# Scores over 192 keys in two query halves, tiles at multiples of 64 bytes, and a new order in the opening of a one-core transformer layer

## The chip, the cores and the metric

The kernel runs on one core of one Trainium2 chip. The metric is the device time of one execution in microseconds (us), as the median of several executions. The kernel before takes 1698.69 us (median of 3, 1698.04 to 1703.2).

## The reference, cut to what matters

One layer over 2048 tokens of width 1024. `c` sets a shift, a scale and a gate per channel; the input is modulated, multiplied by one wide matrix, cut into eight pieces, and two token mixers (windowed attention with sinks, and a causal pool) are gated, added, projected and normalised.

```python
mod = jax.nn.silu(c) @ w_ada[l] + b_ada[l]               # 1024 -> 3 * 1024
shift, scale, gate = jnp.split(mod, 3, axis=-1)
u = x * (1.0 + scale[:, None, :]) + shift[:, None, :]
q, k, v, a_gate, p_in, p_gate, m_a, m_p = jnp.split(u @ w_in[l], offsets, axis=-1)
# attention: 16 query heads, 2 key heads, head width 64; query i sees keys i-127 .. i
logits = q k^T / 8 + bias[bucket(i - j)];  masked outside the window
probs = softmax(concat(logits, sink_of_head))[..., :-1]   # the sink takes weight, has no value
a = (probs @ v) * silu(a_gate) @ w_attn_proj
p = (group_linear(pool(p_in)) * pool_scale) * silu(p_gate) @ w_pool_proj
y = (sigmoid(m_a) * a + sigmoid(m_p) * p) @ w_out * (1 + gate)
x = LayerNorm(alpha * x + y)
```

The kernel is given float32 and keeps about that precision: each operand of a product is split into a rounded part and the rest ("hi" and "lo", type fp32r), and three matmuls (hi*hi, hi*lo, lo*hi) stand for one.

## The kernel before, in words

**Products.** Every large product of the layer is a 2x2 block product done with seven block products instead of eight (Strassen's way, in Winograd's form). The seven names of the moving operand are B11, T1, T2, B21, T3, B22 and T4; each is a set `set_<name>` in SBUF of 4 pieces of 128 rows by 512 columns, hi and lo. A `Quad` is one 2x2 block product: two weight matrices of 128 columns each over 1024 rows against 1024 tokens. Its weights go through four stages, F (B11, T1), S (T2, B21), Th (T3, B22) and L (T4). Each of the seven products is `product()`: 4 pieces times 3 matmuls, 12 matmuls of 128x512 on TensorE, which accumulate in a PSUM bank (`mm`, or `lg` and `c` for pairs of quads). A weight is split by a cast on ScalarE (`w_set<-W`, CAST) and a subtraction on VectorE (`w_set<-W,w_set`); GpSimd forms the sums of weights (`W<-W`).

**Phases.** The tokens are done in two halves, s = 0 and 1. For each half: a start phase (`g0`, `g1`) with the quads for keys/values, the first queries and two gates; the phase "alone" (`o0`, `o1`), in which 13 quads run one after another and the attention is laid over them; and an end phase (`e0`, `e1`), in which pool jobs are laid over four pairs of quads. Then come the projections, `w_out` and the LayerNorms.

**What sets the order.** `plan()` writes all products down in one list and places the loads and the splits of weights some products ahead; `run()` walks it, and `at`, `defer` and `steps` hang other work at a position in it. All engines run in that program order; the tile framework adds the waits. Each engine has one queue, SyncE (SP) issues nearly all DMAs.

**Attention in "alone".** `overlay()` cuts it into 128 steps a layer (64 for each half of the tokens: 8 pairs of heads times 8 blocks of 128 queries). `step(n)` is called after every 4.7 groups of three matmuls or so and does parts of four steps at once: the score matmuls of step n (`scores`: for each of two heads, hi and lo, 128 queries against 256 keys, into the only `lg` bank), the four transposes of step n-2 into the only `pt` bank, and the four matmuls with the values of step n-3 (`pv`). Behind them ScalarE divides the weights of step n-1 by their sum, casts `pt` to `pth`, copies half of `pv` to `o`, and takes two exponentials; VectorE takes a reciprocal, adds bias and takes the minimum with the sink (`CUSTOM_DVE_ANT_0 L<-lg,bt,nsink`), then forms `ptl<-pt,pth`, then adds the two halves of `pv`. The transposes of a step must wait until the `ptl` of the step before has read the one `pt` bank. `load_q` fetches the queries of two steps, two steps ahead, from `q_d`; `q_quad.consume` writes `q_d` from a ring of 5 (4 in the second half) tiles of the tag `c`.

**The opening.** `head()` writes the order of the first two quads (keys/values and queries, F and S) out by hand. A row of `mod` for 128 channels comes in two ways: shifts on TensorE (`pe_modulation`: eight matmuls with one moving column, "a list" below), scales on VectorE (`modulation`: `head_T<-head_T,cb,mod` over 1024 elements), which needs `cb`, silu(c) on every partition. `cb` is c read by a broadcasting DMA, put through tanh on ScalarE and two operations of VectorE. For channel tiles 0 to 3 that gives B11 and T1, for 4 to 7 B21 and T2; from them come T3, B22 and T4. `idle_products` are matmuls on constants that keep TensorE's clock up. Then `first_start` lays 16 "folds" over the rest of the phase (`fold_parts`: the pool's mix matrix times the pool's columns of `w_in`, 12 matmuls of 128x256 each), and the gates' rows of `mod` (`gate_modulation`).

The lines of most instructions in the profile are one helper's (L56), so groups are told apart by their tiles' names.

## Time and profile before

| what | us |
| --- | --- |
| median of three executions | 1698.69 |
| the profiled execution, device time | 1703.35 |
| its span in the trace | 1701.2 |
| TensorE busy | 1665.3 |
| VectorE, ScalarE, GpSimd busy | 1185.1, 988.4, 589.4 |

Up to about 161 us the start phase of the first half runs, from 161 to 480 us the first "alone" phase, from 740 to 1060 us the second; the rest are phases without attention. The PE rows count a matmul from its start until its result is out, so the times of matmuls that follow each other overlap: the group row's busy time divided by its count is what one of them costs in a row of its kind.

### The profile page before, as it was taken

Reading aid. Unit: us, or ns where it says so; the run is one execution under the profiler, and the core shown is the slowest. Engines: PE = TensorE matmul, PEld = TensorE weight load, DVE = VectorE, ACT = ScalarE, POOL = GpSimd, SP = SyncE. Lnnn points to the kernel's source line nnn. Section 1 sums busy time; section 2 is a strip of 40 time slices with the busy share of each in tenths; the row PEclk is TensorE's granted clock in tenths of the full one; section 3 lists DMA queues with packets and bytes.
Section 4 is the critical chain, followed back from the end, with each engine's and each line's share of the span. In section 5 each row is a group of like instructions: output and inputs, shape, how many; then the busy total and the mean of one; then the engine's idle time right before and its main releaser. Section 6 shows DMA issues by size and latency. Waiting matters only on the chain.

```text
span 1701.2 us, 24948 instructions
## 1 busy us (share of the span) xinstructions
PE 1665.3 (98%) x8112; PEld 1397.0 (82%) x8112; DVE 1185.1 (70%) x2167; ACT 988.4 (58%) x1943; POOL 589.4 (35%) x563
## 2 busy tenths in 40 slices
PE   9899999999999999999999999999999999999997
PEld 7788888888788888888888888888888888888886
DVE  6855666666647778656666666487876785778878
ACT  4645888787853336358877787333544453434553
POOL 3013454545462223323424333322242211113544
PEclk9899999999999999999999999999999999999999
DMA  9489676776557889865456454589968685777343
GB/s 358 151 294 311 202 225 217 242 239 208 170 178 223 264 288 326 289 206 157 150 171 215 156 175 135 190 280 326 329 238 309 197 312 201 261 264 281 149 149 124
DMA packets 236833, 389.50 MB, mean 229 GB/s; under 512 B 20872, under 2 KB 90528, under 8 KB 236576
## 3 DMA queue, kind: packets, MB, share of 16 engines
q1 hardware_dynamic: 231280, 382.36, 66.8%
q10 hardware_dynamic: 5392, 5.53, 1.0%
q8 instruction: 64, 1.05, 0.3%
q14 instruction: 65, 0.53, 0.1%
q0 software_dynamic: 32, 0.02, 0.0%
HBM read 243.63 MB, written 147.35 MB: 230 GB/s over the span
## 4 chain that ended last, share of the span: by engine, by line
PE 68%; ACT 11%; DVE 6%; issue 5%; DMA 3%; POOL 1%; SPq 1%; DVEq 0%; ACTq 0%; POOLq 0%
PE mm L56 43%; PE lg L56 11%; PE c L56 9%; ACT L L56 5%; PE pv L56 3%; PE pt L56 3%; DVE w_set L56 2%; ACT pth L56 2%; ACT w_set L56 1%; DVE wide L56 1%; ACT sig L56 1%; DVE p L56 1%; DVE ptl L56 1%; SPq L56 1%; ACT q_hi L56 0%
## 5 line engine op out<-in xcount | busy, mean ns | idle before, releaser
L56 PE MATMUL mm<-set_B,w_set 128*128 128x512 f32 x2664 | 652.7, 391 | 0.6 <-DVE w_set L56 0.6
L56 PEld LDWEIGHTS mm<-set_B,w_set 128*128 128x128 f32 x2664 | 496.6, 188 | 103.7 <-DVE w_set L56 1.5
L56 PE MATMUL mm<-set_T,w_set 128*128 128x512 f32 x1896 | 466.1, 392 | 1.5 <-POOL w_set L56 1.2
L56 POOL TENSOR_TENSOR W<-W 128x512 f32<-128x512 f32 x185 | 266.9, 1453 | 573.1 <-DVE w_set L56 394.0
L56 PEld LDWEIGHTS mm<-set_T,w_set 128*128 128x128 f32 x1896 | 351.5, 189 | 74.4 <-POOL w_set L56 2.5
L56 DVE TENSOR_TENSOR w_set<-W,w_set 128x1024 fp32r<-128x1024 f32 x197 | 254.5, 1292 | 110.5 <-ACT w_set L56 109.2
L56 ACT ACTIVATE L<-L 128x257 f32<-128x257 f32 (+3 forms) x512 | 241.4, 498 | 96.8 <-DVE L L56 96.3
L56 ACT CAST w_set<-W 128x1024 fp32r<-128x1024 f32 x222 | 232.2, 1047 | 97.2 <-PE mm L56 54.2
L56 PE MATMUL lg<-set_T,w_set 128*128 128x512 f32 x828 | 201.0, 391 | 2.7 <-ACT lg L56 1.7
L56 PE MATMUL c<-set_T,w_set 128*128 128x512 f32 x828 | 200.8, 391 | 0.0
L56 PEld LDWEIGHTS lg<-set_T,w_set 128*128 128x128 f32 x828 | 155.4, 188 | 36.2 <-ACT lg L56 2.1
L56 PEld LDWEIGHTS c<-set_T,w_set 128*128 128x128 f32 x828 | 155.8, 189 | 32.2
L56 DVE TENSOR_TENSOR ptl<-pt,pth 128x512 fp32r<-128x512 f32 (+1 forms) x128 | 86.4, 675 | 112.6 <-ACT pth L56 112.6
L56 POOL TENSOR_TENSOR W<-W,A 128x512 f32<-128x512 f32 x41 | 57.9, 1412 | 275.1 <-DMA A<-in_win_dram 102.7
L56 DVE CUSTOM_DVE_ANT_0 L<-lg,bt,nsink 128x256 f32<-128x256 f32 (+1 forms) x256 | 110.1, 467 | 25.1 <-PE lg L56 20.9
L56 ACT ACTIVATE sig<-mm 128x512 f32<-128x512 f32 x76 | 45.5, 599 | 94.6 <-PE mm L56 92.5
L56 PEld LDWEIGHTS lg<-kk,qs 128*128 128x128 f32 x512 | 77.4, 189 | 15.4 <-DVE L L56 4.6
L56 PE MATMUL pt<-ident,L 128*128 128x128 f32 x496 | 76.7, 276 | 9.3 <-DVE ptl L56 8.8
L56 PE MATMUL lg<-kk,qs 128*128 128x256 f32 (+1 forms) x512 | 81.5, 281 | 2.2 <-DVE L L56 1.9
L56 POOL TENSOR_TENSOR w_set<-W,w_set 128x1024 fp32r<-128x1024 f32 x25 | 61.0, 2441 | 63.7 <-ACT w_set L56 37.5
L56 PE MATMUL pv<-pth,vv 128*128 128x256 f32 x248 | 74.8, 323 | 1.1 <-DMA vv<-v_d 1.1
L56 DVE TENSOR_TENSOR st<-pv,o 64x128 f32<-64x128 f32 x256 | 71.3, 279 | 5.5 <-ACT o L56 3.8
(207 smaller groups left out, 1884.2 us busy)
## 6 DMA issues: line engine op xcount, KB each, us to landing
W<-in_win_dram SPq DMA_DIRECT2D x40, 512.0 KB, 5.8
qs<-q_d SPq DMA_DIRECT2D x128, 128.0 KB, 4.3
sums_d<-W SPq DMA_DIRECT2D x62, 256.0 KB, 4.1
W<-sums_d SPq DMA_DIRECT2D x31, 512.0 KB, 4.2
ain_d<-st SPq DMA_DIRECT2D x56, 256.0 KB, 3.5
A<-in_win_dram SPq DMA_DIRECT2D x42, 256.0 KB, 5.6
q_d<-q_hi SPq DMA_DIRECT2D x32, 256.0 KB, 4.4
q_d<-q_lo SPq DMA_DIRECT2D x32, 256.0 KB, 4.2
```

The lines of the kernel that those rows point to most:

```text
L56: return lambda *args, **kw: self.tc.keep_in_program_order(op(*args, **kw))
```

## The change

**Scores.** A block of 128 queries of two heads is no longer taken as two heads of 128 queries, but as two halves of 64 queries, each with both heads stacked on the 128 partitions. A half needs only 192 keys (`BAND`): keys 0 to 191 of the window's 256 for the first half, 64 to 255 for the second. So the four score matmuls of a step have 192 columns in place of 256 (in the first block of the sequence 64 and 128 in place of 128), and bias-and-minimum, exponential and division work on 192 or 193 columns in place of 256 or 257. The bias tile is 192 wide and loaded by two DMAs, the sink is one value per partition. The transposes and the matmuls with the values keep their size: the 64 columns that a half doesn't use are zeroed once for each of three fixed rooms for `L`. `q_d` is laid out in blocks of 64 queries, so that its DMAs move pieces of 64 floats.

**Tiles.** A room for `L` is 528 floats in place of 518, so the tiles allocated behind it start at multiples of 64 bytes.

**Seeds.** In the end phases both accumulators of the first pair get a matmul that opens the bank (one more for each of two phases).

**Opening.** `cb` is made on TensorE (silu(c)'s columns, broadcast as weights, against the identity) and copied by ScalarE; the DMA, the tanh and two VectorE operations for it go. The scales of channel tiles 5 and 6 are done on TensorE as well. The hand-written order of F and S is another, the Th products of the first two quads are woven (T3, T3, B22, B22 in place of T3, B22, T3, B22), some consumers of these quads come up to five products later (`LATER`), and the 16 folds start four products later; the last eight come two to a product.

```diff
-    nsink = cp.tile([P, HEADS], F32, name="nsink")
+    nsink = cp.tile([P, 2 * KT], F32, name="nsink")[:, :KT]
...
-    q_d = dp.tile([2, KT, 2, 2, P, CH], F32, name="q_d")
+    q_d = dp.tile([2, KT, 2, 2, CH // HD, P, HD], F32, name="q_d")
...
-            self.fresh = True
+            self.fresh = {0, 1} if "pg" in bufs else {1}
...
+                    if kind == "Th" and gi == 0 and phase.get("woven"):
...
+                        products += [(q, kind, h, name) for h, name in enumerate(names) for q in grp]
+                        continue
...
+    LATER = {(0, "S"): 5, (1, "S"): 4, (1, "Th"): 5, (1, "L"): 2}
...
+    def keep_q(dst, x):
+        sp.dma_start(dst.rearrange("b p c -> p b c"), x.rearrange("p (b c) -> p b c", c=HD))
...
+        rooms = [tp.tile([P, 2 * 257 + 14], F32, tag=f"L{i}", bufs=1, name="L") for i in range(3)]
+        for room in rooms:
+            pool.memset(room[:, 1 + BAND : 1 + BAND + P], 0.0)
...
-            q = qts[h] = tp.tile([P, 2, 2 * P], F32R, tag="qs", bufs=2, name="qs")
+            q = qts[h] = tp.tile([P, 4, 2, HD], F32R, tag="qs", bufs=2, name="qs")
             for n in range(2):
-                src = q_d[s, j, t, n][:, c * 2 * P : (c + 1) * 2 * P].rearrange("(h d) c -> d h c", h=2)
-                sp.dma_start(as32(q[n * HD : (n + 1) * HD]), src)
+                src = q_d[s, j, t, n, 4 * c : 4 * c + 4].rearrange("b (h d) c -> d (b h) c", h=2)
+                sp.dma_start(as32(q[n * HD : (n + 1) * HD]).rearrange("p b h c -> p (b h) c"), src)
...
+        def span_of(n, eo):
+            k0 = k0_of(n)
+            return (max(k0, HD), 2 * P) if eo else (k0, BAND)
...
         def scores(n):
...
-            for h in range(2):
+            for eo in range(2):
+                whi = q[:, n % 2 * 2 + eo].rearrange("p h c -> p (h c)")
+                k0, k1 = span_of(n, eo)
                 for hl in range(2):
                     mm(
-                        lg[:, h, k0:],
-                        q[:, h, at : at + P],
-                        kvt["k"][:, hl, (b - 1 + s) * P + k0 : (b + 1 + s) * P],
+                        lg[:, eo, k0:k1],
+                        whi,
+                        kvt["k"][:, hl, (b - 1 + s) * P + k0 : (b - 1 + s) * P + k1],
...
-                        L[:, h, e0:256],
-                        lg[:, h, e0:],
-                        bts[j][:, h, e0:],
+                        L[:, a:c],
+                        lg[:, eo, k0:k1],
+                        bts[j][:, k0 - HD * eo : k1 - HD * eo],
...
+                    with_sink = L[:, a : c + 1] if eo else L[:, a - 1 : c]
...
-        sp.dma_start(cb, c.partition_broadcast(P))
...
-        act.activation(late[0], cb, AF.Tanh, scale=0.5)
-        dve.tensor_scalar(late[0], late[0], 0.5, 0.5, ALU.mult, ALU.add)
-        dve.tensor_tensor(cb, cb, late[0], ALU.mult)
+        for h in range(2):
+            row = bank(("pv", "pt")[h])
+            for i in range(KT // 2):
+                k = h * (KT // 2) + i
+                mm(row[:, i * P : (i + 1) * P], ct[:, k : k + 1].to_broadcast([P, P]), ident, start=i == 0, stop=True, skip_group_check=True)
+            act.copy(cols(cb, h), row)
...
+    PE_SCALE = (5, 6)
...
+            for n in range(2 if k in PE_SCALE else 1):
+                for i in range(KT):
+                    at_i = slice(i * P, (i + 1) * P)
+                    mm(sums[k][:, n : n + 1], ws[k][n][:, at_i], ct[:, i : i + 1], start=i == 0, stop=i == KT - 1)
```

The first place is TensorE in `head()`, where the S products of the first pair begin (`lg` and `c` with T2, `mm` with B21; the rows `ct,head_...` are the lists, eight matmuls with one moving column each; the two single rows with 128x512 open the banks). Before:

```order
L56 MATMUL mm<-set_B_66,w_set 128x512 x3
L56 MATMUL mm<-set_T_67,w_set 128x512 x3
L56 MATMUL pv<-ct,head_big 128x1 x8
L56 MATMUL lg<-set_B_66 128x512
L56 MATMUL c_463<-set_B_66 128x512
L56 MATMUL lg<-set_T_159,w_set 128x512 x3
L56 MATMUL mm<-set_B_68,w_set 128x512 x3
L56 MATMUL pt<-ct,head_big_112 128x1 x8
L56 MATMUL c_463<-set_T_159,w_set 128x512 x3
```

And after the change:

```order
L56 MATMUL mm<-set_B_66,w_set 128x512 x3
L56 MATMUL mm<-set_T_67,w_set 128x512 x3
L56 MATMUL lg<-set_B_66 128x512
L56 MATMUL c_435<-set_B_66 128x512
L56 MATMUL pt<-ct,head_B_116 128x1 x16
L56 MATMUL pv<-ct,head_big 128x1 x16
L56 MATMUL lg<-set_T_159,w_set 128x512 x3
L56 MATMUL mm<-set_B_68,w_set 128x512 x3
L56 MATMUL c_435<-set_T_159,w_set 128x512 x3
L56 MATMUL mm<-set_B_68,w_set 128x512 x3
L56 MATMUL pt<-ct,head_big_112 128x1 x8
```

Four lists (two tiles, shift and scale) now stand in one block between the last F product and the first S product, where one list of tile 6 stood; the list of tile 5 stood between F products.

The second place is TensorE behind it, the Th and L products of the first pair (T3 is `set_T_406` before and `set_T_411` after, B22 `set_B_565` and `set_B_459`, T4 `set_T_621` and `set_T_613`; `vt` rows transpose the values, `spare,room_w` rows are folds). Before:

```order
L56 MATMUL lg<-set_T_406,w_set 128x512 x12
L56 MATMUL mm<-set_B_565,w_set 128x512 x12
L56 MATMUL pt<-ident,vt 128x128 x4
L56 MATMUL c_463<-set_T_406,w_set 128x512 x12
L56 MATMUL pv<-spare,room_w 128x256 x12
L56 MATMUL mm<-set_B_565,w_set 128x512 x12
L56 MATMUL pt<-spare,room_w 128x256 x12
L56 MATMUL lg<-set_T_621,w_set 128x512 x12
L56 MATMUL pv<-spare,room_w 128x256 x12
L56 MATMUL c_463<-set_T_621,w_set 128x512 x12
L56 MATMUL pt<-spare,room_w 128x256 x12
L56 MATMUL pv<-ident,vt 128x128 x4
```

And after:

```order
L56 MATMUL lg<-set_T_411,w_set 128x512 x12
L56 MATMUL c_435<-set_T_411,w_set 128x512 x12
L56 MATMUL mm<-set_B_459,w_set 128x512 x12
L56 MATMUL pt<-ident,vt 128x128 x4
L56 MATMUL mm<-set_B_459,w_set 128x512 x12
L56 MATMUL lg<-set_T_613,w_set 128x512 x12
L56 MATMUL c_435<-set_T_613,w_set 128x512 x12
L56 MATMUL pv<-ident,vt 128x128 x4
```

No fold stands here any more, and one more product stands between the first T3 product and the first transposes of `vt`.

The third place is TensorE at the start of the first "alone" phase. Before:

```order
L56 MATMUL lg<-kk,qs 128x128 x4
L56 MATMUL mm<-set_T_406,w_set 128x512 x9
L56 MATMUL mm<-set_B_565,w_set 128x512 x6
L56 MATMUL lg<-kk,qs 128x256 x4
L56 MATMUL mm<-set_B_565,w_set 128x512 x6
```

And after:

```order
L56 MATMUL lg<-kk,qs 128x64 x2
L56 MATMUL lg<-kk,qs 128x128 x2
L56 MATMUL mm<-set_T_411,w_set 128x512 x9
L56 MATMUL mm<-set_B_459,w_set 128x512 x6
L56 MATMUL lg<-kk,qs 128x192 x4
L56 MATMUL mm<-set_B_459,w_set 128x512 x6
```

The products and the places of the steps among them are the same; only the width of the score matmuls differs.

## The prediction

> **What bounds the kernel now.** I read the page's totals first, then the busy times by stage, then what TensorE waited for, then the rows of the opening in order of time.

> ```profile
> PE 1665.3 (98%) x8112; PEld 1397.0 (82%) x8112; DVE 1185.1 (70%) x2167; ACT 988.4 (58%) x1943; POOL 589.4 (35%) x563
> ```

> TensorE is the bound: 36 us of the span of 1701.2 are not busy. So only two kinds of gain exist: less TensorE work, and less of these 36 us (or of the time in which TensorE runs slowly). By stage (busy us of PE, PEld, DVE, ACT, POOL, then granted clock, DMA share, GB/s):

> ```profile
> 200.00:300.00 100.00, 97.64 (x539) 83.16 (x538) 63.03 (x196) 84.19 (x211) 50.28 (x58) 1.00 0.68 222
> 740.00:900.00 160.00, 158.00 (x869) 135.69 (x868) 103.99 (x298) 125.59 (x309) 51.33 (x63) 1.00 0.54 172
> 1060.00:1660.00 600.00, 599.13 (x2642) 495.18 (x2641) 446.90 (x507) 266.62 (x364) 173.17 (x124) 1.00 0.71 248
> ```

> Where attention is laid over the products (first two rows) ScalarE is busy for about 80% and TensorE loses 1 to 2%; behind it (last row) TensorE loses nearly nothing. What TensorE waited for (total, times, longest):

> ```profile
> PE pt L56 <- DVE ptl L56: 8.8, 17, 0.7
> PE pt L56 <- ACT vt L56: 3.2, 1, 3.2
> PE pv L56 <- DVE room_small L56: 2.2, 1, 2.2
> PE lg L56 <- DVE L L56: 1.9, 3, 0.9
> PE lg L56 <- ACT lg L56: 1.7, 1, 1.7
> PE pv L56 <- DVE spare L56: 1.1, 1, 1.1
> PE pv L56 <- ACT spare L56: 1.0, 1, 1.0
> ```

> `ptl` and `L` are waits of the attention steps, 10.7 us; the others, 9.2 us, lie in the opening.

> **Scores.** The groups of score matmuls, whole and in the sequence's first block (count | busy, mean ns of one), and what VectorE and ScalarE do behind them:

> ```profile
> L56 PE MATMUL lg<-kk,qs 128*128 128x256 f32 x480 | 76.9, 283 | 1.9 <-DVE L L56 1.9
> L56 PE MATMUL lg<-kk,qs 128*128 128x128 f32 x32 | 4.6, 265 | 0.3 <-DMA qs<-q_d 0.3
> L56 DVE CUSTOM_DVE_ANT_0 L<-lg,bt,nsink 128x256 f32<-128x256 f32 x240 | 105.2, 475 | 22.8 <-PE lg L56 18.6 <-POOL L L56 3.8
> L56 DVE CUSTOM_DVE_ANT_0 L<-lg,bt,nsink 128x128 f32<-128x128 f32 x16 | 4.9, 342 | 2.3 <-PE lg L56 2.3
> L56 ACT ACTIVATE L<-L 128x257 f32<-128x257 f32 x240 | 120.5, 505 | 2.8 <-DVE L L56 2.4 <-POOL L L56 0.4
> L56 ACT ACTIVATE L<-L 128x129 f32<-128x129 f32 x16 | 6.3, 399 | 2.3 <-DVE L L56 2.3
> ```

> Four matmuls of 256 columns hold TensorE for 76.9/120 = 0.64 us, four of 128 for 4.6/8 = 0.575 us: half the columns save a tenth. The time per matmul hardly follows the columns, so something else, nearly constant, sets it. 192 columns lie between: the saving of a step is 0 to 0.066 us, 0 to 8 us over 120 steps. I take the middle of the two rows, 0.033 us a step: 4 us.

> [...]

> **Stalls of the attention steps.** The chain in a step is reciprocal, two divisions and `pth` on ScalarE, `ptl` on VectorE, transposes on TensorE; ScalarE does them in its queue behind the exponentials of the step before and the casts of the products. An exponential goes from 505 ns at 257 columns to 399 at 129, 0.83 ns a column, so 64 columns save 53 ns; the divisions have the same width less one. Four of them: 0.21 us of ScalarE a step. VectorE saves (475-342)/128 x 64 = 66 ns, twice a step. The chain of one step becomes about 0.2 us shorter. If lateness comes from one step alone, each of the 20 waits (17 + 3) shrinks by 0.21 us, 4.2 us in all; if ScalarE carries it over steps, all 10.7 us can go. ScalarE is at 80%, so queues build up over more than one step: I take 6.

> **Alignment and seeds.** Behind the old room of 518 floats (2072 bytes) lie, among others, the ring of one split weight that only this phase has, `pth`, `ptl` and the tiles `c`. No row prices the address. The nearest rows are 12 matmuls in the attention phase and 12 before it:

> ```profile
> 199.72 2.96 PE L56 MATMUL mm<-set_T,w_set 128*128 128x512 f32 x12
> 63.54 2.88 PE L56 MATMUL mm<-set_B,w_set 128*128 128x512 f32 x12
> ```

> 0.08 us a product, 182 products, of which one weight buffer in five is a moved one: 0 to 3 us, I take 1. Two more seed matmuls cost 0.23 us each, 0.5 us.

> **Opening.** TensorE's rows (start, length):

> ```profile
> 7.98 1.92 PE L56 MATMUL pv<-ct,head_T 128*128 128x1 f32 x16 [0.21 <-DMA head_T<-in_wadat_dram]
> 9.75 5.97 PE L56 MATMUL lg<-set_B 128*128 128x512 f32 x18
> 15.57 1.84 PE L56 MATMUL pt<-ct,head_T 128*128 128x1 f32 x16
> 43.19 0.96 PE L56 MATMUL lg<-set_T,w_set 128*128 128x512 f32 x3 [1.69 <-ACT lg L56]
> 45.17 3.41 PE L56 MATMUL pt<-ct,head_big 128*128 128x1 f32 x16
> 60.82 2.88 PE L56 MATMUL lg<-set_T,w_set 128*128 128x512 f32 x12
> 69.62 0.63 PE L56 MATMUL pt<-ident,vt 128*128 128x128 f32 x4 [3.20 <-ACT vt L56]
> 83.82 1.59 PE L56 MATMUL pv<-spare,room_w 128*128 128x256 f32 x12
> 89.79 2.99 PE L56 MATMUL mm<-set_B,w_set 128*128 128x512 f32 x12
> 94.96 2.66 PE L56 MATMUL pv<-spare,room_w 128*128 128x256 f32 x12 [2.17 <-DVE room_small L56]
> ```

> Prices: a list takes 1.77 us from start to start (7.98 to 9.75) at full clock and 3.4 at half (the row at 45.17); a product 2.72 (60.82 to 63.54), so 0.227 a matmul; a row's length has 0.16 more than that, so a fold is 1.59 - 0.16 = 1.43.

> *Until S begins.* In VectorE's rows silu(c)'s column is ready, and `cb` after it:

> ```profile
> 3.22 0.17 DVE L56 TENSOR_TENSOR ct<-ct,sg 128x8 f32<-128x8 f32 x1
> 9.77 1.28 DVE L56 CUSTOM_DVE_ANT_0 head_T<-head_T,cb,mod 128x1024 f32<-128x1024 f32 x1 [0.57 <-DMA head_T<-in_wada_dram]
> 10.98 0.15 DVE L56 TENSOR_TENSOR mod<-mod,pv 128x1 f32<-128x1 f32 x1
> ```

> After: from 3.4, eight fp32 matmuls for `cb` (the list's eight show as 16 records; at half clock 3.4 us) to 6.8, eight idle ones at half clock (0.43 each) to 10.2, list 0 to 12.0. So the first shift is 1 us later than at 10.98. Then 18 idle ones (4.1 to 5.8 us) and, in the new order, lists 1 to 4 (7.1), 48 product matmuls, 6 idle, 2 seeds (56 x 0.227 = 12.7) and the double lists 5 and 6 (7.1): S begins at 12.0 + 5 + 26.9 = 43.9, 0.7 later than before. VectorE keeps up: four more scale products (1.21 from row to row), four split weights (as long), about 20 operations of 0.6 us and some 6 us of waits for ScalarE end near 40.

> *The clock.* Granted clock in stretches of 3.41 us, PE alone:

> ```profile
> 6.56:9.97 3.41, 3.20 (x22) 1.00 0.99 396
> 9.97:13.38 3.41, 3.41 (x9) 0.50 1.04 407
> 40.69:44.10 3.41, 1.72 (x9) 1.00 0.40 157
> 44.10:47.51 3.41, 3.41 (x16) 0.50 0.02 7
> ```

> The stretch at 6.56 was "busy" for 3.20, yet more than half of it with a list, and half clock follows: lists don't count as work. In the new order four of them stand in a block of 6.8 us, so half clock must come within it. About half the block then costs double (+3.4), the first S pieces too (+2.7), list 7 (+1.7), and the following pieces until one whole stretch is full (+1.7 to 2.6): S, which takes 2.7 + 1.7 + 8.2 = 12.6 at full clock, ends at 43.9 + 12.6 + 9.5 = 66.0 in place of 60.82: 5.2 later.

> *Behind S.* Before, from 60.82 to 89.79 are 28.97 us for six products (16.3), two sets of transposes (0.8) and four folds (5.7): 6.2 us of waits, 3.20 of them before the transposes, and 2.8 more follow at 94.96 with the half clock it brings. After, the wait for `vt` has another product before it, no fold stands here, and VectorE's list (T3, third weights, B22, T4: about 24 operations of 0.6 us in 17 us) leaves about 1 us of waiting: 8 gained. The 16 folds keep their price further on. Opening: 8 - 5 = 3 gained; bounds 12 (clock stays full) and -2 (half clock through all of S, waits as before for half).

> **Sum.** 4 + 6 + 1 - 0.5 + 3 = 13.5 us. The profiled span goes from 1701.2 to 1687.7; the profiled execution (1703.35) was 4.7 above the median, so on the median's scale 1698.7 - 13.5 = 1685.

> **Rivals.** *The score matmuls pay by the column* (10%): 64 columns at the rate of the product row (0.227 us for 512) are 28 ns, 480 times 13.6 us in place of 4: 1675.5. For it: products do pay so; against it the 128-column row.

> *The clock stays full in the opening* (15%): 9.5 us better, 1675.7. Against it the stretches above; for it only that their bounds may fall otherwise.

> *Nothing but the matmuls is gained* (12%): the steps' waits are set by the casts of the products and stay, the opening loses 2: 4 + 1 - 0.5 - 2 = 2.5, 1696, no change.

> *The small pieces of `q_d` come late* (8%, slower). Packets and landing times:

> ```profile
> q1 hardware_dynamic: 231280, 382.36, 66.8%
> q10 hardware_dynamic: 5392, 5.53, 1.0%
> q_d<-q_hi SPq DMA_DIRECT2D x32, 256.0 KB, 4.4
>   DMA q_d<-q_hi: 0.5, 1
> ```

> A q quad casts into a ring of 5 (or 4) tiles, so its third result waits for the store of the first; the last row, the wait in ScalarE's queue, says that 4.4 us just suffices. Twice that would hold ScalarE, and all steps queued behind it, for some 4 us twice in each of 6 quads: up to 48 us, of which its idle fifth hides little; with half of it 1685 + 24 = 1709. It decides from a landing of about 6 us. Against it: a packet takes 66.8% x 16 x 1701 / 231280 = 79 ns at 1653 bytes on the first queue and 50 ns at 1026 on the second, so 256 bytes come to some 15 ns, 1024 of them on 16 engines to 1 us, 0.4 more than now. [...]

> **Numbers.** The forecast has 55%, with 1679 to 1692 as its own range. The range takes in the two faster rivals and most of "nothing": 1669 to 1696. A change of 0.3% (5.1 us) is about what measurements of this kernel can tell. Faster by more: forecast, both faster rivals and little of the third, 0.82; same 0.11; slower 0.07.

> **What would show it.** Right: score groups of four near 0.61 us; waits of `pt` for `ptl` about halved; half clock in the opening for 10 to 17 us; no wait for `vt`, first fold without one; 10.7 us of step waits at about 5. Wrong: score groups at 0.5 us, a clock of 1.00 through 60 us, ScalarE waiting for `q_d`, or new waits of TensorE for DMAs around 75 to 150 us, where the DMA share is already near 1.

## The result and the profile after

The changed kernel takes 1685.78 us (median of 4 runs, 1685.5 to 1688.98); the kernel before, run beside it, 1699.76 (median of 4, 1698.04 to 1703.2). The ratio is 0.992, with a 95% interval of 0.9899 to 0.994: about 14 us, 0.8%, faster. The profiled span went from 1701.2 to 1683.8 us, 17.4 less; the profiled execution of the kernel before was a long one of its kind, so a little of the 17.4 is that.

The totals of the page after:

```profile
PE 1654.8 (98%) x8146; PEld 1392.7 (83%) x8146; DVE 1164.9 (69%) x2161; ACT 962.7 (57%) x1944; POOL 588.4 (35%) x569
```

ScalarE lost 25.7 us of work and VectorE 20.2; TensorE's busy time fell by only 10.5. The other 6.9 us of the 17.4 are idle time of TensorE, 36 before and 29 now. The groups of the attention steps (count | busy, mean ns of one):

```profile
L56 PE MATMUL lg<-kk,qs 128*128 128x192 f32 x480 | 71.2, 270 | 2.3 <-DMA qs<-q_d 1.6 <-DVE L L56 0.7
L56 DVE CUSTOM_DVE_ANT_0 L<-lg,bt,nsink 128x192 f32<-128x192 f32 x240 | 89.2, 410 | 19.1 <-PE lg L56 18.5
L56 ACT ACTIVATE L<-L 128x193 f32<-128x193 f32 x240 | 107.6, 452 | 2.9 <-DVE L L56 2.3 <-POOL L L56 0.6
L56 ACT ACTIVATE L<-L 128x192 f32<-128x192 f32 x240 | 96.4, 451 | 89.0 <-DVE L L56 88.5
```

Four score matmuls cost 71.2/120 = 0.593 us in place of 0.641; an exponential 452 ns in place of 505. What TensorE waited for (total, times, longest):

```profile
PE pt L56 <- DVE ptl L56: 5.4, 14, 0.7
PE pv L56 <- DVE mod L56: 4.5, 1, 4.5
PE lg L56 <- DMA qs<-q_d: 2.9, 2, 1.6
PE c L56 <- DVE q_lo L56: 1.4, 1, 1.4
PE lg L56 <- DVE L L56: 0.7, 2, 0.5
```

`ptl` and `L` together went from 10.7 us to 6.1. The waits for `vt`, `spare` and `room_small` are gone. New are 4.5 us at the very start, until `mod` and the columns of silu(c) are there (the kernel before waited 1.5 us there, for `set_B`), 1.4 us for `q_lo` in the opening, and 2.9 us for the first queries `qs` of the two attention phases. By stage (busy us of PE, PEld, DVE, ACT, POOL, then granted clock, DMA share, GB/s):

```profile
200.00:300.00 100.00, 99.03 (x555) 85.27 (x556) 62.75 (x199) 82.92 (x216) 49.01 (x57) 1.00 0.72 207
740.00:900.00 160.00, 159.06 (x892) 137.49 (x891) 103.00 (x306) 124.78 (x323) 54.65 (x65) 1.00 0.62 170
```

In the first stretch TensorE loses 0.97 us of 100 where it lost 2.36, though ScalarE is busy for 82.9 us of it, after 84.2: the stretch now holds more of the work.

TensorE's rows of the opening and of the two phase starts, after (start, length):

```profile
35.86 4.71 PE L56 MATMUL pt<-ct,head_B 128*128 128x1 f32 x32
40.43 6.96 PE L56 MATMUL pv<-ct,head_big 128*128 128x1 f32 x32
47.26 1.63 PE L56 MATMUL lg<-set_T,w_set 128*128 128x512 f32 x3
62.16 0.61 PE L56 MATMUL lg<-set_T,w_set 128*128 128x512 f32 x2
75.68 2.55 PE L56 MATMUL lg<-set_T,w_set 128*128 128x512 f32 x10 [0.58 <-DVE w_set L56]
159.07 0.63 PE L56 MATMUL lg<-kk,qs 128*128 128x64 f32 x4 [1.34 <-DMA qs<-q_d]
732.13 0.66 PE L56 MATMUL lg<-kk,qs 128*128 128x192 f32 x4 [1.61 <-DMA qs<-q_d]
```

and the phase starts before:

```profile
161.69 0.63 PE L56 MATMUL lg<-kk,qs 128*128 128x128 f32 x4 [0.25 <-DMA qs<-q_d]
743.33 0.71 PE L56 MATMUL lg<-kk,qs 128*128 128x256 f32 x4
```

The first scores mark three stretches: the opening (to the first score of the first attention phase), from there to the first score of the second, and from there to TensorE's last matmul (read as starts of matmuls from the trace; 1691.6 us before, 1673.8 after). Opening 161.7 to 159.1: 2.6 us gained. First attention phase with what follows it 581.6 to 573.1: 8.6. The second with all that follows 948.2 to 941.7: 6.6.

Inside the two attention phases (first score to last value matmul, 642.4 us before, 626.0 after) the intervals between the starts of TensorE's matmuls split the 16.4 us gained about like this (a wait is what an interval has above the median of its kind): 6.2 on the score matmuls, last one included (5.7 by the rows above); 4.5 on waits ahead of transposes (13.2 to 8.7 us); 1.7 on waits ahead of score groups; 1.4 on one wait for values `vv`; 1.6 on a stretch of half clock at 457 us which followed a wait and did not come again; the rest, a microsecond, is spread. Some of the gain was given back at the start of the second phase, where the queries come 1.6 us late.

### The profile page after: what moved, and what is told of

Its sections match the earlier page's. It is cut to its first block, busy times and chain, and to the rows that moved or that the text cites. A ratio compares the mean times of both kernels' runs of the same rounds, so it can differ in the third digit from the quotient of the medians.

```text
span 1683.8 us, 24835 instructions
## 1 busy us (share of the span) xinstructions
PE 1654.8 (98%) x8146; PEld 1392.7 (83%) x8146; DVE 1164.9 (69%) x2161; ACT 962.7 (57%) x1944; POOL 588.4 (35%) x569
## 5 line engine op out<-in xcount | busy, mean ns | idle before, releaser
L56 PE MATMUL mm<-set_B,w_set 128*128 128x512 f32 x2664 | 651.5, 391 | 0.7 <-DVE w_set L56 0.7
L56 PEld LDWEIGHTS mm<-set_B,w_set 128*128 128x128 f32 x2664 | 496.1, 188 | 103.5 <-DVE w_set L56 1.5
L56 POOL TENSOR_TENSOR W<-W 128x512 f32<-128x512 f32 x185 | 268.0, 1459 | 584.2 <-DVE w_set L56 344.9
L56 PE MATMUL mm<-set_T,w_set 128*128 128x512 f32 x1896 | 463.7, 391 | 1.0 <-POOL w_set L56 0.7
L56 PEld LDWEIGHTS mm<-set_T,w_set 128*128 128x128 f32 x1896 | 349.7, 188 | 73.1 <-POOL w_set L56 1.9
L56 DVE TENSOR_TENSOR w_set<-W,w_set 128x1024 fp32r<-128x1024 f32 x197 | 255.5, 1297 | 107.6 <-ACT w_set L56 93.0
L56 ACT CAST w_set<-W 128x1024 fp32r<-128x1024 f32 x222 | 232.2, 1047 | 95.5 <-PE mm L56 55.6
L56 ACT ACTIVATE L<-L 128x193 f32<-128x193 f32 (+5 forms) x512 | 214.9, 446 | 99.5 <-DVE L L56 98.4
L56 PE MATMUL lg<-set_T,w_set 128*128 128x512 f32 x828 | 201.4, 391 | 1.4 <-DVE w_set L56 1.0
L56 PE MATMUL c<-set_T,w_set 128*128 128x512 f32 x828 | 200.8, 390 | 0.0
L56 PEld LDWEIGHTS lg<-set_T,w_set 128*128 128x128 f32 x828 | 155.1, 188 | 34.9 <-DVE w_set L56 1.8
L56 PEld LDWEIGHTS c<-set_T,w_set 128*128 128x128 f32 x828 | 155.5, 188 | 33.0 <-DVE w_set L56 0.8
L56 DVE TENSOR_TENSOR ptl<-pt,pth 128x512 fp32r<-128x512 f32 (+1 forms) x128 | 86.4, 675 | 117.5 <-ACT pth L56 117.5
L56 POOL TENSOR_TENSOR W<-W,A 128x512 f32<-128x512 f32 x41 | 58.1, 1418 | 271.1 <-DMA A<-in_win_dram 106.6
L56 DVE CUSTOM_DVE_ANT_0 L<-lg,bt,nsink 128x192 f32<-128x192 f32 (+2 forms) x256 | 93.6, 404 | 22.3 <-PE lg L56 21.7
L56 ACT ACTIVATE sig<-mm 128x512 f32<-128x512 f32 x76 | 45.5, 599 | 92.8 <-PE mm L56 89.8
L56 PEld LDWEIGHTS lg<-kk,qs 128*128 128x128 f32 x512 | 76.2, 190 | 15.7 <-issue 4.2
L56 POOL TENSOR_TENSOR w_set<-W,w_set 128x1024 fp32r<-128x1024 f32 x25 | 60.9, 2435 | 77.8 <-ACT w_set L56 69.4
L56 PE MATMUL pt<-ident,L 128*128 128x128 f32 x496 | 76.5, 275 | 5.7 <-DVE ptl L56 5.4
L56 PE MATMUL lg<-kk,qs 128*128 128x192 f32 (+2 forms) x512 | 75.8, 270 | 3.6 <-DMA qs<-q_d 2.9
L56 POOL TENSOR_TENSOR st<-st,ag 128x512 f32<-128x512 f32 x32 | 46.5, 1452 | 84.3 <-DVE st L56 78.5
L56 ACT CAST pth<-pt 128x512 fp32r<-128x512 f32 (+1 forms) x128 | 71.9, 562 | 6.4 <-PE pv L56 5.6
## 6 DMA issues: line engine op xcount, KB each, us to landing
sums_d<-W SPq DMA_DIRECT2D x62, 256.0 KB, 3.6
ain_d<-st SPq DMA_DIRECT2D x56, 256.0 KB, 3.6
A<-in_win_dram SPq DMA_DIRECT2D x42, 256.0 KB, 5.5
q_d<-q_hi SPq DMA_DIRECT2D x32, 256.0 KB, 4.1
q_d<-q_lo SPq DMA_DIRECT2D x32, 256.0 KB, 3.9
```

Of the source, the lines that this page charges most:

```text
L56: return lambda *args, **kw: self.tc.keep_in_program_order(op(*args, **kw))
```

## The experiments

Theory: the gain comes from the attention steps; ScalarE's queue carries lateness from step to step, so its shorter exponentials and divisions are worth more than the shorter matmuls; the opening gives a few microseconds, limited by half clock. Rivals: the columns of the score matmuls pay; the addresses pay; the opening's gain is the main one. Each run's profile gives the three stretches named above (us), and the timed median stands beside them:

| kernel | opening | to second phase | to the end | median | ratio to before, interval |
| --- | --- | --- | --- | --- | --- |
| before | 161.7 | 581.6 | 948.2 | 1700.4, 1701.66, 1700.75 | |
| changed | 159.1 | 573.1 | 941.7 | 1685.78 | 0.992, 0.9899 to 0.994 |
| e1 attention part | 164.5 | 571.9 | 942.9 | 1690.8 | 0.9938, 0.9921 to 0.9954 |
| e2 opening part | 160.6 | 580.8 | 949.0 | 1701.52 | 1.0003, 0.9993 to 1.0012 |
| e3 ScalarE as wide as before | 161.8 | 584.1 | 947.2 | 1702.29 | 1.0012, 1.0003 to 1.0022 |
| e4 scores as wide as before | 164.6 | 574.0 | 944.9 | 1689.64 | 0.9937, 0.9922 to 0.9953 |
| e5 room of 518 | 162.9 | 572.2 | 943.6 | 1689.58 | 0.9922, 0.9908 to 0.9935 |
| e6 scales on VectorE | 160.8 | 571.7 | 943.2 | 1684.71 | 0.9898, 0.9884 to 0.9912 |
| e7 idle matmuls between lists | 161.0 | 572.6 | 942.0 | 1688.94 | 0.9922, 0.9908 to 0.9937 |
| e8 steps four beats later | 164.6 | 575.9 | 945.3 | 1692.41 | 0.9947, 0.9932 to 0.9961 |
| e9 changed, again | 159.0 | 572.9 | 942.5 | 1686.55 | 0.9918, 0.9904 to 0.9931 |
| e10 q before k | 158.3 | 573.2 | 941.9 | 1687.42 | 0.992, 0.9907 to 0.9932 |
| e11 as e6 | 158.5 | 571.4 | 943.0 | 1684.81 | 0.9907, 0.9894 to 0.9921 |
| e12 e10 and e11 | 159.5 | 571.3 | 942.5 | 1686.05 | 0.9912, 0.99 to 0.9925 |

(e1 to e4, e5 to e8 and e9 to e12 shared a chip and its runs of the kernel before: the three medians of the first row.)

The three stretches come from one profile each, and the first of them is the least firm: the changed kernel, e9, e3, e5 and e4 have the same order of the opening, and their first score comes at 159.1, 159.0, 161.8, 162.9 and 164.6 us. A difference of 2 or 3 us in that column alone shows nothing.

**The two halves of the change apart.** e1 is the kernel before with the edits on scores, tiles and seeds; e2 is the kernel before with those on the opening.

```diff
# e1: the attention's edits, two places of them; the opening as before
+        rooms = [tp.tile([P, 2 * 257 + 14], F32, tag=f"L{i}", bufs=1, name="L") for i in range(3)]
...
+            return (max(k0, HD), 2 * P) if eo else (k0, BAND)
...
# e2: the opening's edits, two places of them; the attention as before
+    LATER = {(0, "S"): 5, (1, "S"): 4, (1, "Th"): 5, (1, "L"): 2}
...
+    PE_SCALE = (5, 6)
```

> Only the attention's part of the change (192 keys, rooms, layout of the queries, seeds), with the opening as before. My reading of the two traces: from the first to the last step the two attention phases got 9.9 and 6.5 us shorter, the point where they start came 2.6 us earlier. If the two parts add, this kernel has the 16.4 us less a late start of the second phase: 14 to 16 us below the kernel before. The rival, that the earlier and different opening is what unties the attention steps, expects less than 8 us here.

> Only the opening's part, with attention over 256 keys as before. If the parts add: 2 to 3 us below the kernel before, the first score matmul near 159 us in place of 161.7, TensorE's waits in the attention steps as before (about 11 us). The rival expects the attention phases to be shorter here too.

Measured: e1 gains 0.62% (10.5 us; 14 to 16 were expected), e2 nothing that can be told (its interval reaches from 0.07% faster to 0.12% slower). e1's two attention stretches are those of the whole change, to about a microsecond. Its opening is 2.8 us longer than the one of before, in the same order: in that execution TensorE waited 2.2 us for `head_T` from DRAM, and half clock followed from 22 to 29 us. In e2 the attention phases, measured as above, take 641.5 us, as before (642.4), so the new opening does not untie the steps. So the attention edits carry the gain. What the opening adds to them is left open: alone it is worth nothing within 2 us, and the whole change is 3.4 us faster than e1 (0.9918 against 0.9938) with intervals that overlap.

**ScalarE's width against TensorE's.** e3 lets the exponentials and divisions run over 257 and 256 columns again, 64 of them outside the half's 192 keys (the softmax then runs over these columns too), while score matmuls and VectorE stay at 192. e4 does the reverse: score matmuls over 256 columns, of which 64 are not read, and ScalarE at 193 and 192.

```diff
# e3
+                    if not k0_of(n - 1):
+                        k0, k1 = 0, 2 * P
                     x = E[:, 1 + 2 * P * eo + k0 : 1 + 2 * P * eo + k1]
...
+                    if not k0_of(n):
+                        with_sink = L[:, 257 * eo : 257 * eo + 257]
# e4
                 k0, k1 = span_of(n, eo)
+                if not k0_of(n):
+                    k0, k1 = 0, 2 * P
                 for hl in range(2):
```

> The changed kernel, but ScalarE's exponentials and divisions run over 257 and 256 columns again, the zeroed ones included (which makes the softmax wrong, and leaves all else as it is); score matmuls and VectorE's minimum stay at 192. Theory: the steps' stalls come from ScalarE's queue, so the time in which TensorE is held in the steps goes from about 10 us back to about 20 and the kernel is 6 to 10 us slower than the changed one, with score groups still at 0.59 us. Rival (VectorE's shorter minimum, or the new layout, removed the stalls): under 2 us slower.

> The changed kernel, but the score matmuls have 256 columns again (64 of them are read by nobody); ScalarE and VectorE stay at 192. If the width is worth what the traces say of the groups of four (0.64 against 0.59 us), 5 to 6 us slower than the changed kernel; if columns were paid in full (28 ns for 64), 13 us; if a shorter score group only feeds a longer wait, 0 to 2 us.

Measured: e3 loses the whole gain (1.0012, about 16 us more than the changed kernel, where 6 to 10 were expected), e4 keeps 10.7 us of it (0.9937). An exponential of e3, and the first waits of its page:

```profile
L56 ACT ACTIVATE L<-L 128x257 f32<-128x257 f32 x240 | 120.4, 505 | 3.0 <-DVE L L56 2.6 <-POOL L L56 0.4
PE pt L56 <- DVE ptl L56: 12.0, 20, 0.8
PE lg L56 <- DMA qs<-q_d: 5.3, 3, 3.0
```

and the rows of e4 for the same wait and for its score group:

```profile
PE pt L56 <- DVE ptl L56: 3.1, 9, 0.7
L56 PE MATMUL lg<-kk,qs 128*128 128x256 f32 x480 | 76.7, 283 | 1.7 <-DMA qs<-q_d 1.0 <-issue 0.6
```

With the two kernels of the comparison this is a square for the wait of the transposes for `ptl`:

| | ScalarE 257 columns | ScalarE 193 columns |
| --- | --- | --- |
| scores 256 columns | 8.8 (before) | 3.1 (e4) |
| scores 192 columns | 12.0 (e3) | 5.4 (after) |

Narrowing ScalarE takes 5.7 or 6.6 us off this wait; narrowing the matmuls puts 3.2 or 2.3 us on it: TensorE reaches the transposes sooner, and ScalarE is no sooner done. Each cell is one profile, but the differences are larger than what profiles of the same attention code differ by: the corner of the kernel before has 7.7 in e2, the corner of the changed kernel 4.7 to 5.7 in the eight others that leave the steps as they are (e1, e5 to e7, e9 to e12). So 5.5 us fewer of score matmuls (76.7 to 71.2) are worth about 3 us: e4's attention phases take 630.4 us in place of 626.0, 1.5 of it half clock at a phase start, and its ratio is 0.0017 to 0.0019 above the changed kernel's, with intervals that overlap. (The kernel before has VectorE at 256 columns and the old opening too, so its corner is not quite clean.) In e3 the loss has a second part that the theory did not name: the queries of the first phase came 3.0 us late and 6.8 us of half clock followed (start, length):

```profile
161.79 1.09 PE L56 MATMUL lg<-kk,qs 128*128 128x64 f32 x4 [2.98 <-DMA qs<-q_d]
162.67 4.15 PE L56 MATMUL mm<-set_T,w_set 128*128 128x512 f32 x9
```

Nine matmuls took 4.15 us where they take 2.3 at full clock; a second stretch of half clock followed at 458 us, where the kernel before had one. Of the 16.2 us by which e3's attention phases are longer than the changed kernel's, some 8 are waits ahead of transposes, 4.4 half clock and 1.4 waits ahead of score groups. Why the queries came later in e3 is not known.

**Addresses.** e5 gives the rooms their old 518 floats, with all other edits kept.

```diff
-        rooms = [tp.tile([P, 2 * 257 + 14], F32, tag=f"L{i}", bufs=1, name="L") for i in range(3)]
+        rooms = [tp.tile([P, 2 * 257 + 4], F32, tag=f"L{i}", bufs=1, name="L") for i in range(3)]
```

> The changed kernel with rooms of 518 floats for L, so that the tiles behind them start 32 bytes off a multiple of 64 again. By intervals between product matmuls in the two traces (under 1 us over both phases) it should make no difference that can be told: 0 to 1 us slower. If placing were a main part of the gain, 4 us or more.

Measured: 0.9922 against 0.992 and 0.9918 for the changed kernel, no difference. In the trace a product's matmul takes about 0.3 ns longer in the first attention phase and 0.5 in the second (229.9 and 230.0 ns on average from start to start, where the changed kernel has 229.6 and 229.5), 0.7 us over the some 1900 such intervals. The address is worth a microsecond at most.

**The opening's clock.** e6 moves the scales of channel tiles 5 and 6 back to VectorE, so that the double lists become single ones; e7 keeps the changed order and puts nine matmuls on constants ahead of three of the lists.

```diff
# e6
-    PE_SCALE = (5, 6)
+    PE_SCALE = ()
...
         pe_modulation(5)
+        scale_sum(5)
# e7
+                if k in PE_SCALE and (k, n) != (5, 0):
+                    t = sets["B11"][:, 0, 0, :]
+                    for _ in range(9):
+                        mm(sums[k][:, 2:], t[:, 0:P], t[:, 2:], start=True, stop=True, skip_group_check=True)
```

> The changed kernel, but the scales of channel tiles 5 and 6 are done on VectorE as before. Theory: in the opening the block of four lists holds TensorE from 35.9 to 47.3 us (half of it at half clock) while the sets of the first S pieces are ready at 40.6, and VectorE waits 3 us twice for the lists. With two lists the block ends at about 40.5, S ends near 57 in place of 62.8, and VectorE, which has two more scale products (2.4 us), still ends its lists earlier. The Th products start 4 to 5 us earlier; the whole is 2 to 5 us faster than the changed kernel. Rival: VectorE's list is what bounds S and Th, so 2 us slower.

> The changed kernel with nine idle matmuls of 510 columns ahead of the second, third and fourth list of the block (6 us of added work for TensorE). Theory: lists count for nothing in what sets TensorE's clock, so with idle matmuls between them the clock stays at 1.00 through the opening: the block takes 7.1 + 6.1 us in place of 11.4, S starts at 49 in place of 47.3 but runs at full clock and ends at 61.5, 1 us before the changed kernel's. If lists do count, or the clock falls for another reason, half clock stays and S ends 6 us later.

In e7 the clock is full from about 8 to 97 us (granted 1.00 from 36.18 to 62.39, the lists, the fillings and S). Its rows of one of the three fillings, of the start of S and of its end:

```profile
37.88 2.35 PE L56 MATMUL pt<-set_B 128*128 128x510 f32 x9
49.57 0.96 PE L56 MATMUL lg<-set_T,w_set 128*128 128x512 f32 x3
62.39 0.61 PE L56 MATMUL lg<-set_T,w_set 128*128 128x512 f32 x2
```

S ends at 62.39, in the changed kernel at 62.16: three fillings of 2.2 us cost the 6.6 us that the half clock had cost, and the time is no better. In e6 S ended at 59.6 and the median is the lowest of the four that shared its chip, yet its first score came at 160.8. The changed kernel and e6 once more, side by side on one chip:

> The changed kernel itself, on the chip of the next three runs, so that they have a base beside them. Its profile showed waits for q of 1.5 and 1.8 us at the starts of the two attention phases and one wait of 0.6 us for a split weight at 75 us; the runs with the same opening showed 1.0 to 3.0 us and 1.7 us there. Expected: a ratio to the kernel before between 0.990 and 0.994; attention phases of 312.8 and 313.2 us again; S from 47 to 62 us.

> The kernel of e6 (the scales of the last two sums by VectorE instead of TensorE) beside the changed kernel of e9. In e6 S ended at 59.6 us in place of 62.2, but first scores came at 160.8 against 159.1. Theory: the lists cost what their half clock costs and nothing hides them, so 2 to 3 us faster than e9 (ratio 0.998 to it). Rival: what is won before S is given back in waits for split weights between 62 and 160 us: the same as e9 within 1.5 us, and e6's 0.9898 was a draw.

The changed kernel's rows in e9, a second profile of the same program:

```profile
36.26 3.63 PE L56 MATMUL pt<-ct,head_B 128*128 128x1 f32 x32
39.75 5.42 PE L56 MATMUL pv<-ct,head_big 128*128 128x1 f32 x32
45.03 1.63 PE L56 MATMUL lg<-set_T,w_set 128*128 128x512 f32 x3
59.33 0.61 PE L56 MATMUL lg<-set_T,w_set 128*128 128x512 f32 x2
73.97 2.56 PE L56 MATMUL lg<-set_T,w_set 128*128 128x512 f32 x10 [1.71 <-DVE w_set L56]
159.00 0.63 PE L56 MATMUL lg<-kk,qs 128*128 128x64 f32 x4 [2.40 <-DMA qs<-q_d]
```

The same lists now meet 6.8 us of half clock in place of 13.7, and S ends 2.8 us sooner. Yet the first score comes at the same time: 1.1 us more go into the wait for a split weight at 74 us, 0.6 more into the one for `q_lo` at 93 us (2.1 us in all) and 1.1 more into the one for `qs`: 2.8 us, all that S won. e11 is 1.7 us faster than e9 in the medians (1684.66 to 1686.25 against 1686.16 to 1688.12), 0.1%, with intervals of the ratios that overlap; the theory said 2 to 3 us, and S ended hardly sooner in it (59.12 against 59.33). The scales on VectorE are a better choice by a microsecond or two at most; why is not settled.

**The late queries.** e8 lets the attention steps begin four beats (of three matmuls) later; e10 issues the loads of the queries ahead of those of the keys; e12 is e10 with e11.

```diff
# e8
-        state = [0, 0.0, 12]
+        state = [0, 0.0, 16]
# e10, e12
-        load_k(0)
         load_q(0)
+        load_k(0)
```

> The changed kernel with the first attention step of each phase 4 groups of three matmuls later (16 in place of 12). At both phase starts TensorE waits for the first queries (1.3 and 1.6 us), which land some 8 us after their DMA. 4 groups are 2.7 us: both waits go, nothing else is late, since the steps leave room at the end of the phase: 2 to 3 us faster than the changed kernel. If the wait only moves to the next load (keys of the second head group, values), no difference.

> The two loads of q are issued ahead of the loads of k at the start of each attention phase. Theory: the waits for q (3.3 us in the changed kernel's profile, 2.6 to 5.3 in the others) come from the place in SyncE's queue; q is issued 1.2 us earlier in the first phase and 2.5 us earlier in the second, so the waits shrink by 1.2 and 1.8 us: about 3 us faster than e9. Rival: the loads share transfer engines that are 99% busy there (window 140 to 165 us), k lands as late as q did, the wait only changes its name: the same time as e9.

> The edits of e10 and e11 together. If both theories hold, 5 us faster than e9; if both rivals hold, the same as e9; if one, 2 to 3 us.

e10's first scores wait as long as e9's, only for the other load:

```profile
158.25 0.64 PE L56 MATMUL lg<-kk,qs 128*128 128x64 f32 x4 [2.15 <-DMA kk<-k_d]
```

So the order of these two loads is not the cause, and e12 adds nothing to e11 either. The transfer engines are full there in both kernels (DMA share 1.02 from 140 to 160 us before, 1.00 after). The packets in the traces show what fills them just then: the keys come in 128 packets of 8192 bytes, some 0.55 us each. In the changed kernel these move from 150.7 to 156.9 us and the queries' packets from 155.0 to 158.1; in e10 the queries' move first, from 148.8 to 151.2, and the keys' until 157.1. The first scores need both, and TensorE, which now arrives sooner, finds one of them still on its way. The change has also cut the queries' loads from packets of 1024 bytes to packets of 256. No run tests that alone, but e2, which has the old packets behind the new opening, waits 1.2 us for its first queries too, and in e10 it is the keys, whose packets are as before, that TensorE waits for.

e8 was to gain 2 to 3 us and is slower than the changed kernel (0.9947 against 0.992 and 0.9918). In e8 the waits at the phase starts are gone, but TensorE waits for queries in the middle of both phases, 2.0 and 3.6 us, and half clock follows each time. Its row of TensorE, and what SyncE's queue waited for from 805 to 822 us:

```profile
826.54 0.67 PE L56 MATMUL lg<-kk,qs 128*128 128x192 f32 x4 [3.58 <-DMA qs<-q_d]
```

```profile
SPq L56 <- POOL L L56: 7.0, 2, 6.7
SPq L56 <- ACT L L56: 6.0, 1, 6.0
```

SyncE stands for 6.7 us behind GpSimd and issues two pairs of query loads 2.8 us apart; over the two phases a pair comes about every 10 us. The stretches from phase start to phase start and to the end are 2.9 and 3.7 us longer than in the changed kernel, and the first phase starts later by design. A later start of the steps is no gain. That it moves the loads of the queries to a worse place in SyncE's order is how these rows read; no run shows it by itself.

No version was found that beats the changed kernel by more than e6 and e11 do.

## Why the prediction was right, and where its terms were not

The forecast was 1685, measured was 1685.78; the forecast case is the one that came, and none of the rivals. The terms of the attention part (4 + 6 + 1 - 0.5 = 10.5 us) agree with e1, which has that part alone: 10.5 us by the ratio, 9.6 by the medians. That it is so close is partly luck: the profiles have 3.0 us that the sum left out, and e1's opening lost 2.8. The 3 us of the opening are not shown: e2, the opening alone, gains 1 us at most by its interval. The sum, term by term, from the profiles:

| term | predicted | measured |
| --- | --- | --- |
| score matmuls | 4 (0 to 8) | 5.7 by the page's rows, 6.2 by intervals |
| waits of the steps | 6 (4.2 to 10.7) | 4.6 by the page's rows, 6.2 by intervals |
| values and half clock at 457 us | not in the sum | 3.0 |
| alignment | 1 (0 to 3) | under 1 (e5) |
| seeds | -0.5 | not measured apart |
| opening | 3 (-2 to 12) | 2.6, 2.7 (e9), -1.2 (e5), -2.9 (e4); timed alone 0 (e2) |
| late queries in the second phase | not in the sum | -1.6 |

**Scores.** The middle between the rows of 128 and 256 columns gave 0.61 us a group; 0.593 came. The cost is not straight between the rows: from 128 to 192 columns a matmul gains (0.593 - 0.575)/4 = 4.5 ns, from 192 to 256 it gains 12. From start to start inside a group the trace of before has 98 ns on average at 128 columns and 120 at 256 (medians of 114, 119 and 120 for the three intervals), the one of after 105 at 192 (88, 113 and 112). What sets the cost at 192 columns and below no run shows. The rival "columns paid in full" (28 ns a matmul) is refuted by e4's row.

**Waits of the steps.** That ScalarE's width sets these waits is what e3 and e4 show. That lateness is carried from step to step fits too: ScalarE's relief takes 6.6 us off e3's 20 waits for `ptl`, and 20 times the 0.21 us of one step are only 4.2. What the step missed is that it took the two savings as independent: narrower matmuls alone make the wait longer by 2 to 3 us, and ScalarE's relief alone is worth 5.7 to 6.6 us in the row for `ptl`. The net of 4.6 us in the rows of the page lay between the two cases (4.2 and 10.7) and near the lower. The prediction looked for `pt` waiting half as long; it was 5.4 in place of 8.8. "About 5" for the 10.7 us was 6.1. The rival "nothing but the matmuls" is refuted by the same runs: e3, which has the shorter matmuls and not ScalarE's relief, is no faster than the kernel before, though half clock is part of its loss.

**Opening.** That the profile's 2.6 us are near the 3 of the sum is luck: both parts of the sum are wrong. S was to begin at 43.9 at full clock and to end at 66.0, 5.2 later; it began at 47.3 and ended at 62.2, 1.3 later. At full clock the block of four lists would have ended at 35.86 + 7.1 = 43.0; half clock added 4.3 to the block and 2.3 to S, 6.6 in all, where 9.5 were put. List 7 ran at full clock (1.84 us) and the clock was full again after the first stretch full of products, so the term that was mis-sized is the half clock; its length, 13.7 us, was inside the 10 to 17 named, but the 6.8 us of e9 were not. The start itself was 1 us later than the 3.4 us of the prediction: the sinks, one value per partition now, are loaded by two DMAs, which ScalarE issues ahead of the work on silu(c), so the attention part of the change costs the opening this 1 us. (The block of lists still began at 35.86, 0.9 sooner than the prediction's terms add up to.) The changed kernel, and below it e2, where one DMA loads them:

```profile
3.78 0.21 ACT L56 ACTIVATE sg<-ct 128x8 f32<-128x8 f32 x1 [1.54 <-issue]
```

```profile
2.78 0.21 ACT L56 ACTIVATE sg<-ct 128x8 f32<-128x8 f32 x1 [0.56 <-DMA ct<-in_ccol_dram]
```

Behind S 8 us were to be won; from the end of S to the first score it took 100.9 us before and 96.9 after: 4.0, and in e9 1.2. The waits that were named did go (`vt`, the first fold), but others came: split weights at 75 us (0.6 us, 1.7 in most other runs), `q_lo` at 94 us (1.4), `st` (0.9) and the queries at 159 us. The step "VectorE's list leaves about 1 us of waiting" failed. The rival "the clock stays full", 9.5 us better, did not come, and its price looks too high: in e9, with half of the half clock, S ended 2.8 us sooner and the first score came no sooner. e7 can't settle that price, since its fillings cost TensorE as much as the half clock had.

**Small pieces of `q_d`.** The stores were not late:

```profile
q1 hardware_dynamic: 334880, 376.99, 69.8%
q_d<-q_hi SPq DMA_DIRECT2D x32, 256.0 KB, 4.1
q_d<-q_lo SPq DMA_DIRECT2D x32, 256.0 KB, 3.9
```

104 thousand more packets than before take three points more of the transfer engines' span, and a store lands in 4.1 us where it took 4.4. The rival's point of decision, 6 us, was not near. The late transfers of this change were loads, the first `qs` of a phase, now also in pieces of 256 bytes, and the prediction did not look for them: it listed waits for DMAs only up to 150 us.

## What to carry to other kernels

Where one engine is nearly full and a second serves it through a queue, price a change of both as a square of four cases, not as a sum: here the faster TensorE work lengthened the wait by 2.3 or 3.2 us, and the relief of ScalarE, busy for 58% of the span before, took 5.7 or 6.6 us off it. Time won ahead of a stretch whose loads keep the transfer engines full (DMA share 1.03 from 140 to 160 us in e9) can reappear as a wait at the first tile that these loads bring, as all of e9's 2.8 us did in part at that wait and in part at two waits before it; read the DMA share of the stretch into which a gain is to be carried before booking it.
